# Weights split one chunk ahead, a third block of the MLP in seven products, and the scheduler's order at both ends of the MLP

## The chip, the cores and the metric

The kernel runs on one core of one Trainium2 chip. The metric is the device time of one execution in microseconds (us), lower is better. The time before is the median of three runs.

## The reference

A two-layer transformer for one sequence of T = 256 tokens, width D = 2048, all in float32. Layer 0 mixes with stick-breaking attention, layer 1 with native sparse attention; each is followed by an MLP with 4 x 2048 = 8192 hidden channels.

```python
def sqrelu_mlp(h, w1, w2):
    return jnp.square(jax.nn.relu(h @ w1)) @ w2

def reference(x, ...):
    h = x
    for layer in range(DEPTH):                    # DEPTH = 2
        if layer % N_MIXERS == 0:
            h = h + stick_breaking_attention(rms_norm(h, ...), sb_w_qkv, sb_w_out)
        else:
            h = h + native_sparse_attention(rms_norm(h, ...), nsa_w_in, ..., nsa_w_out)
        h = h + sqrelu_mlp(rms_norm(h, mlp_norm_g[layer]), mlp_w1[layer], mlp_w2[layer])
    return h
```

The change touches the two MLPs and the few microseconds before and behind them.

## The kernel before

**Chunks.** All weights stream through the core once, in chunks of 512 KB: 256 rows of the contraction (KC = 2 tiles of 128) by 512 columns (NB). SP issues the load of a chunk into a `raw` buffer (five) or, in the MLPs, by turns into a `more` buffer (three). A float32 chunk is then split in two: ACT writes the rounded part `hi`, DVE the rest `lo` = raw - hi (function `split`, L143 and L145). There are four buffers of each. PE multiplies hi by both parts of the activations and lo by the high part, so a chunk is three products. With activations x = `xs` (normed input, high and low part) or `yhi`, `ylo` (squared hidden channels) there are three kinds of chunk:

- a chunk of w1 (`chunk_T`, L207): 24 matmuls of 256 columns, 16 with hi and 8 with lo, into two PSUM banks of the pool `acc`;
- a plain chunk of w2 (`chunk_N`, L174): 12 matmuls of 512 columns, 8 with hi and 4 with lo, into two banks of `acc`;
- a seven-product chunk of w2 (`chunk_S`, L270): the chunk's 2 x 2 blocks (two contraction tiles, two halves of the columns) against the 2 x 2 blocks of the activations (two contraction tiles, two halves of the tokens), multiplied as Strassen and Winograd do with 7 products instead of 8: 21 matmuls of 256 columns. DVE first forms four sums of the weight blocks (`ts`, L246 to L250). Three blocks are split as they are (`shi` on ACT, `slo` on DVE, one buffer each), the four sums as a chunk is (`hi<-ts`, `lo<-ts`). The sums of the activations, `ss`, come from the function `high`. The products lie in half banks of four banks of the pool `att`; `add_S` combines them and adds them to h.

**The MLP.** The hidden channels are taken in four groups (fg) of 2048. A group has four blocks of w1 (T, 8 chunks each) and four blocks of w2 (by 512 output columns, nb, 8 chunks each). After a w1 block come the activations: `relu` and `square` on ACT, `high` (ACT and four sums on DVE), `low` and `low7` (ACT and DVE). In groups 0 to 2 blocks 2 and 3 of w2 are seven-product ones, block 0 is plain, and block 1 is half and half: four seven-product chunks in `att`, four plain ones in `acc`. In the last group only block 2 has seven products. When a block is done, `sum2` (plain) or `sum7` (seven-product) adds it to h.

**The order** of PE, DVE, ACT and SP within an MLP is the order in which the code is written (`tc.manual_schedule`); a program's scheduler sets it elsewhere, and POOL's everywhere. `plan` writes it: a list of plain chunks, and a table `after` that says what follows the chunk at each position, a seven-product chunk or a step (a Python call) of the activations and sums. Each group has two lists. The first has w1's blocks 1 to 3 of the group, with the group before's block 3 of w2 among them. The second has block 0 of w2, the next group's block 0 of w1 and the plain chunks of block 1, with the seven-product chunks of blocks 1 and 2 among them. A chunk is loaded, split and multiplied in one go, so that on ACT and DVE its split stands behind every step that was written before its matmuls.

**Work beside it.** While one stage ends, the next one's input is made: `next_x` squares h for the norm (ACT, `junk`, L350), PE transposes h in pieces (`make_x`, L329), ACT and DVE write `xs` from them (L334, L336). `pump` lets one such piece in at the end of each half of a chunk. This happens at the start of an MLP, with the last 512 columns of the stage before, and at the end of the first MLP for the layer that follows.

Of the kernel before, what the change touches and what calls it, by code (L numbers as in the profile page):

```python
# [10 lines left out]
AF = mybir.ActivationFunctionType  # L11
OP = mybir.AluOpType
# [25 lines left out]
JUNK = 1  # L38
SLOPES = [2.0 ** (-8.0 * (i + 1) / NH) for i in range(NH)]
# [3 lines left out]
def hybrid_kernel(  # L43
# [125 lines left out]
    def chunk_N(ps, src, k0, n0, first, last, ahi, alo, koff=0, by_token=False, turn=False):  # L169
# [4 lines left out]
        mm = lambda a, b, k, t, s, e: nc.tensor.matmul(ps[t], a[:, k, t * P:(t + 1) * P], b, start=s, stop=e)  # L174
# [62 lines left out]
    def chunk_S(ps, src, k0, n0, first, last, ahi, alo, shi, slo, koff=0):  # L237

# [13 lines left out]
        thi, tlo = split(ts)  # L252
        k = k0 - koff
# [18 lines left out]
        for i, xh, xl, wh, wl in trivial + sums:  # L272

            mm(i, xh, wh, first and i in (0, 1, 6, 4), False)
            mm(i, xl, wh, False, False)
# [5 lines left out]
    def banks_S(pool, tag):  # L281

        W = NB // 2
        bs = [bank(pool, tag) for _ in range(4)]
        half = lambda j, i: bs[j][:, i * W:(i + 1) * W]
        return bs, [half(0, 0), half(1, 0), half(1, 1), half(2, 0), half(2, 1), half(3, 1), half(3, 0)]

    def add_S(nb, bs, ps, pool, scale):
# [5 lines left out]
        nc.scalar.activation(u[:, 0, :], ps[0], AF.Copy)  # L294
        nc.vector.tensor_tensor(v[:, 0, :], ps[5], u[:, 0, :], op=OP.add)
        nc.vector.tensor_tensor(u[:, 1, :], ps[4], v[:, 0, :], op=OP.add)
        nc.vector.tensor_tensor(v[:, 1, :], ps[6], v[:, 0, :], op=OP.add)
        f0, f1 = scale[:, 0:1], scale[:, 1:2]
        add = lambda o, x, f: nc.vector.scalar_tensor_tensor(o, x, f, o, op0=OP.mult, op1=OP.add)
        add(hb[0], bs[1], f0)  # L300
        add(hb[1], bs[2], f1)
        add(hb[0], u.rearrange("p a n -> p (a n)"), f0)
        add(hb[1].rearrange("p (a n) -> p a n", a=2), v[:, 1, :].unsqueeze(1).to_broadcast([P, 2, W]), f1)
# [114 lines left out]
    def mlp(l, layer, junk, done, last=None):  # L418
# [11 lines left out]
        def chunk1(fg, fb, i):  # L430
            if i == 0:
                banks["T", fb] = [bank(acc, "acc") for _ in range(KB // 2)]
            chunk_T(banks["T", fb], w1, i * KC, fg * D + fb * NB, i == 0, i == NK - 1)
# [33 lines left out]
        def chunk2(fg, nb, i, first, end, turn, by_token=False):  # L467
            if first:
                banks["N", nb] = [bank(acc, "acc") for _ in range(NT)]
            chunk_N(banks["N", nb], w2, fg * KD + i * KC, nb * NB, first, end, yhi, ylo, koff=fg * KD,  # L470
                    by_token=by_token, turn=turn)

        def chunk7(fg, nb, i, first, end):
            if first:
                banks["S", nb] = banks_S(att, "att")
            chunk_S(banks["S", nb][1], w2, fg * KD + i * KC, nb * NB, first, end, yhi, ylo, ss[:, 0], ss[:, 1],
                    koff=fg * KD)

# [3 lines left out]
        def sum7(nb):  # L482
            add_S(nb, *banks["S", nb], junk, factor)

        def plan():
# [17 lines left out]
            def Ss(fg, nb, at, after, ks=range(NK)):  # L503
                for i, j in zip(ks, at):
                    after.setdefault(j, []).append(("S", fg, nb, i, i == ks[0], i == ks[-1]))
# [11 lines left out]
            half = NK // 2  # L517
            for fg in range(NG):
# [683 lines left out]
```

## Time and profile before

| | |
|---|---|
| median of 3 runs | 2160.49 us (2158.95 to 2161.11) |
| the profiled execution's own time | 2155.24 us |
| its span, first to last instruction | 2153.5 us |
| granted TensorE clock, mean | 0.998 |
| busy: PE, DVE, ACT | 2134.2, 1654.2, 1232.2 us |
| moved by DMA | 406.38 MB, mean 189 GB/s |
| seven-product chunks | 136 of 512 in the MLPs |

The span is cut by stages: attention until about 391 us, the first MLP from there to about 1080, the sparse attention to about 1465, and the second MLP to the end. In rows of groups and of the timeline, out<-in are the tiles written and read, then partitions x elements; the number in brackets is the engine's idle time just before and what ended it. Matmuls overlap in their rows (0.28 us for one of 256 columns), so what one costs is read from the starts.

### The profile page before, as it was taken

The page shows a single profiled execution, that of the slowest core. Times are in us where ns is not written, and L with a number is a line of the kernel's source. Part 1 is how long each engine was busy: PE and PEld are TensorE (multiplying, and loading weights), DVE is VectorE, ACT ScalarE, POOL GpSimd, SP SyncE. Part 2 cuts the span into 40 slices and gives each one's busy share as a digit, 9 for nine tenths or more (in the row PEclk, how much of TensorE's full clock was granted, in tenths as well). Part 3 has the DMA queues.
Part 4 walks back from the last instruction along what each step waited for, and adds up shares of the span by engine and source line. Part 5 has one row for each costly group of instructions (what it writes and reads, how often), then busy time and mean ns, then how long its engine had stood idle before and what let it go on. Part 6 is the DMA issues. An engine that isn't in the chain of part 4 may idle for free. (4 is left out here: it accounts for less than half of the span.)

```text
span 2153.5 us, 37647 instructions
## 1 busy us (share of the span) xinstructions
PE 2134.2 (99%) x15110; PEld 1979.8 (92%) x15110; DVE 1654.2 (77%) x2269; ACT 1232.2 (57%) x1683; POOL 45.5 (2%) x78
## 2 busy tenths in 40 slices
PE   9999999999999999999999999999999999999999
PEld 9999988899999999999898888888999999999997
DVE  5556556468989989889687888764589889899896
ACT  6555665455565565565455666654555655655653
POOL 0000000000000000000000100000000000000000
PEclk9999999999999999999999999999999999999999
DMA  7655555566766666666477554455657666666663
GB/s 238 211 169 176 160 182 178 184 202 184 213 196 200 201 205 196 197 214 199 144 197 219 168 145 137 147 189 157 203 185 213 196 200 205 203 197 198 208 214 118
DMA packets 260407, 406.38 MB, mean 189 GB/s; under 512 B 13188, under 2 KB 91912, under 8 KB 260232
## 3 DMA queue, kind: packets, MB, share of 16 engines
q1 hardware_dynamic: 258984, 401.95, 60.6%
q8 instruction: 118, 1.93, 0.4%
q0 software_dynamic: 432, 1.57, 0.2%
q10 hardware_dynamic: 816, 0.46, 0.1%
q14 instruction: 57, 0.47, 0.1%
HBM read 401.83 MB, written 2.10 MB: 188 GB/s over the span
## 5 line engine op out<-in xcount | busy, mean ns | idle before, releaser
L145 DVE TENSOR_TENSOR lo<-raw,hi 128x1024 fp32r<-128x1024 f32 x486 | 590.1, 1221 | 210.8 <-ACT hi L143 201.5
L143 ACT ACTIVATE hi<-raw 128x1024 fp32r<-128x1024 f32 x486 | 509.8, 1054 | 291.5 <-PE acc L174 122.4
L207 PE MATMUL acc<-xs,hi 128*128 128x256 f32 x5360 | 667.3, 277 | 8.3 <-ACT hi L143 7.7
L207 PEld LDWEIGHTS acc<-xs,hi 128*128 128x128 f32 x5360 | 635.9, 188 | 10.2 <-ACT hi L143 8.8
L207 PE MATMUL acc<-xs,lo 128*128 128x256 f32 x2680 | 361.4, 278 | 0.0
L207 PEld LDWEIGHTS acc<-xs,lo 128*128 128x128 f32 x2680 | 331.4, 189 | 0.0
L174 PE MATMUL acc<-hi,yhi 128*128 128x512 f32 x732 | 287.1, 392 | 2.9 <-ACT hi L143 2.9
L174 PE MATMUL acc<-hi,ylo 128*128 128x512 f32 x732 | 285.6, 390 | 0.0
L143 ACT ACTIVATE hi<-ts 128x1024 fp32r<-128x1024 f32 x136 | 144.3, 1061 | 186.8 <-DVE ts L250 185.3
L174 PE MATMUL acc<-lo,yhi 128*128 128x512 f32 x732 | 198.5, 392 | 1.1 <-DVE lo L145 1.1
L145 DVE TENSOR_TENSOR lo<-more,hi 128x1024 fp32r<-128x1024 f32 x129 | 157.4, 1220 | 45.9 <-ACT hi L143 45.2
L145 DVE TENSOR_TENSOR lo<-ts,hi 128x1024 fp32r<-128x1024 f32 x136 | 166.4, 1223 | 23.9 <-ACT hi L143 22.8
L174 PE MATMUL acc<-hi,xs 128*128 128x512 f32 x704 | 177.8, 392 | 0.0
L174 PEld LDWEIGHTS acc<-hi,yhi 128*128 128x128 f32 x732 | 137.4, 188 | 29.4 <-ACT hi L143 3.3
L174 PEld LDWEIGHTS acc<-lo,yhi 128*128 128x128 f32 x732 | 136.5, 188 | 29.8 <-DVE lo L145 2.0
L174 PEld LDWEIGHTS acc<-hi,ylo 128*128 128x128 f32 x732 | 137.5, 188 | 26.0 <-DVE ylo L316 0.2
L143 ACT ACTIVATE hi<-more 128x1024 fp32r<-128x1024 f32 x129 | 135.7, 1052 | 36.3 <-PE acc L207 21.1
L174 PEld LDWEIGHTS acc<-hi,xs 128*128 128x128 f32 x704 | 130.1, 188 | 26.0
L248 ACT ACTIVATE shi<-raw 128x768 fp32r<-128x768 f32 x73 | 61.8, 846 | 103.3 <-PE att L270 103.3
L270 PE MATMUL att<-hi,ss 128*128 128x256 f32 x816 | 114.6, 276 | 0.0
L248 ACT ACTIVATE shi<-more 128x768 fp32r<-128x768 f32 x63 | 53.2, 844 | 97.0 <-PE att L270 97.0
L270 PEld LDWEIGHTS att<-hi,ss 128*128 128x128 f32 x816 | 102.6, 188 | 0.0
(256 smaller groups left out, 2627.5 us busy)
## 6 DMA issues: line engine op xcount, KB each, us to landing
raw<-in_mlp_w_dram SPq DMA_DIRECT2D x320, 512.0 KB, 4.1
more<-in_mlp_w_dram SPq DMA_DIRECT2D x192, 512.0 KB, 4.1
raw<-in_sb_w_qkv_dram SPq DMA_DIRECT2D x95, 512.0 KB, 4.1
raw<-in_nsa_w_in_dram SPq DMA_DIRECT2D x50, 512.0 KB, 3.9
raw<-in_sb_w_out_dram SPq DMA_DIRECT2D x32, 512.0 KB, 4.2
raw<-in_nsa_w_in_dram SPq DMA_DIRECT2D x64, 256.0 KB, 3.8
raw<-in_nsa_w_out_dram SPq DMA_DIRECT2D x32, 512.0 KB, 3.6
w1t<-in_nsa_cmp_w_dram SPq DMA_DIRECT2D x8, 512.0 KB, 4.2
```

What stands on the lines that cost most here:

```text
L143: nc.scalar.activation(hi, raw, AF.Copy)
L145: nc.vector.tensor_tensor(lo, raw, hi.bitcast(F32), op=OP.subtract)
L174: mm = lambda a, b, k, t, s, e: nc.tensor.matmul(ps[t], a[:, k, t * P:(t + 1) * P], b, start=s, stop=e)
L207: nc.tensor.matmul(o, w, x[:, k0 + kk, :], start=s, stop=e, skip_group_check=True)
L248: nc.scalar.activation(hi, flat[:, :3 * W], AF.Copy)
L270: nc.tensor.matmul(ps[i], a, w, start=s, stop=e, skip_group_check=True)
```

## The change

1. `JOINT`: block 1 of w2 in groups 0 to 2 has six seven-product chunks and two plain ones, and the plain ones add to the same banks of `att` (the two whole banks that hold products for one half of the tokens each). One product moves to another half bank for it, and `add_S` makes one addition more in a joint block. The plain block's bank pair for block 1, and its `sum2`, are gone in those groups.
2. `prepare` and `multiply`: the load and split of a chunk are written one chunk ahead of its matmuls, before the steps that follow the chunk in between. Of a seven-product chunk the sums, `shi` and `slo` are written with the chunk before, and its `hi<-ts`, `lo<-ts` behind the split of the next plain chunk.
3. The first eight chunks of w1 in an MLP, and the first MLP's end from position 17 of its last list on (`FREE`), stand in the scheduler's order.
4. `plan`: the next group's block 0 of w1 (eight chunks) now stands behind block 1's plain chunks, and two chunks of the next group's block 1 of w1 follow it; the tables `after` are new. Block 2's last seven-product chunk goes to the next list. In the second MLP's last list `sum2(1)` and `sum7(2)` go one and two positions later.

What the order of the instructions shows. ACT where the first MLP starts; `hi` are the splits of weights, `xs` the next input's pieces, which need PE's transposes, `junk` the squares for the norm. Before:

```order
L143 ACTIVATE hi<-raw 128x1024 x2
L350 ACTIVATE junk,ssq<-h 128x512 x2
L143 ACTIVATE hi<-raw 128x1024
L334 ACTIVATE xs<-att,gT 128x256 x2
L143 ACTIVATE hi<-more 128x1024
L334 ACTIVATE xs<-att,gT 128x256 x2
L143 ACTIVATE hi<-raw 128x1024 x2
```

And now:

```order
L145 ACTIVATE hi<-raw 128x1024 x3
L145 ACTIVATE hi<-more 128x1024
L145 ACTIVATE hi<-raw 128x1024
L366 ACTIVATE junk,ssq<-h 128x512 x2
L145 ACTIVATE hi<-raw 128x1024
L145 ACTIVATE hi<-more 128x1024
L350 ACTIVATE xs<-att,gT 128x256 x2
L145 ACTIVATE hi<-raw 128x1024
L350 ACTIVATE xs<-att,gT 128x256 x2
```

Four more splits stand ahead of the first `xs`; PE's own order is the same there as it was.

ACT at the end of the first MLP, where `uv` is the first step of the sum of block 2. Before:

```order
L294 ACTIVATE uv<-att 128x256
L143 ACTIVATE hi<-raw 128x1024
L350 ACTIVATE junk,ssq<-h 128x512 x2
L143 ACTIVATE hi<-raw 128x1024
L334 ACTIVATE xs<-att,gT 128x256 x4
L143 ACTIVATE hi<-more 128x1024
```

And now:

```order
L145 ACTIVATE hi<-raw 128x1024 x2
L145 ACTIVATE hi<-more 128x1024
L304 ACTIVATE uv<-att 128x256
L145 ACTIVATE hi<-raw 128x1024
L366 ACTIVATE junk,ssq<-h 128x512
L145 ACTIVATE hi<-more 128x1024
L350 ACTIVATE xs<-att,gT 128x256 x4
```

Three splits stand ahead of `uv` now, where one did (the row above the first shown), and the squares are apart.

DVE from block 1's last seven-product chunk (`lo<-ts`) on to block 2, in the first group; `uv` and the `h` rows are the block's sum, `h<-acc` that of block 0. Before:

```order
L145 TENSOR_TENSOR lo<-ts,hi 128x1024
L145 TENSOR_TENSOR lo<-raw,hi 128x1024
L145 TENSOR_TENSOR lo<-more,hi 128x1024
L145 TENSOR_TENSOR lo<-raw,hi 128x1024
L295 TENSOR_TENSOR uv<-att,uv 128x256
L296 TENSOR_TENSOR uv<-att,uv 128x256
L297 TENSOR_TENSOR uv<-att,uv 128x256
L299 SCALAR_TENSOR_TENSOR h<-att,factor,h 128x512 x2
L299 SCALAR_TENSOR_TENSOR h<-uv,factor,h 128x512 x2
L145 TENSOR_TENSOR lo<-more,hi 128x1024
L387 SCALAR_TENSOR_TENSOR h<-acc,factor,h 128x512 x2
L145 TENSOR_TENSOR lo<-raw,hi 128x1024
```

And now:

```order
L147 TENSOR_TENSOR lo<-ts,hi 128x1024
L147 TENSOR_TENSOR lo<-raw,hi 128x1024
L147 TENSOR_TENSOR lo<-more,hi 128x1024
L403 SCALAR_TENSOR_TENSOR h<-acc,factor,h 128x512 x2
L147 TENSOR_TENSOR lo<-raw,hi 128x1024
L306 TENSOR_TENSOR uv<-att,uv 128x256
L307 TENSOR_TENSOR uv<-att,uv 128x256
L309 TENSOR_TENSOR uv<-att,uv 128x256
L310 TENSOR_TENSOR uv<-att,uv 128x256
L302 SCALAR_TENSOR_TENSOR h<-att,factor,h 128x512 x2
L302 SCALAR_TENSOR_TENSOR h<-uv,factor,h 128x512 x2
L249 TENSOR_TENSOR ts<-raw 128x512
```

The sum of block 0 now stands ahead of that of block 1, only three plain chunks' `lo` lie between the two seven-product chunks up to block 2's first sums, and block 1's sum has one row more (L310).

The diff, cut to its core:

```diff
+JOINT = (1,)
+FREE = "the scheduler's order from here"
...
-    def chunk_S(ps, src, k0, n0, first, last, ahi, alo, shi, slo, koff=0):
+    def prepare_S(src, k0, n0):
...
         nc.vector.tensor_tensor(lo, flat[:, :3 * W], hi.bitcast(F32), op=OP.subtract)
-        thi, tlo = split(ts)
+        return hi, lo, ts
+
+    def chunk_S(ps, parts, k, first, last, ahi, alo, shi, slo, starts):
+        W = NB // 2
+        hi, lo, thi, tlo = parts
...
-    def banks_S(pool, tag):
+    def banks_S(pool, tag, joint):
         W = NB // 2
         bs = [bank(pool, tag) for _ in range(4)]
-        return bs, [half(0, 0), half(1, 0), half(1, 1), half(2, 0), half(2, 1), half(3, 1), half(3, 0)]
+        at = [(0, 0), (1, 0), (1, 1), (2, 0), (0, 1) if joint else (2, 1), (3, 1), (3, 0)]
+        return bs, [bs[j][:, i * W:(i + 1) * W] for j, i in at], (0, 1, 6, 3 if joint else 4)
...
+        if joint:
+            nc.vector.tensor_tensor(v[:, 0, :], ps[6], v0, op=OP.add)
+            nc.vector.tensor_tensor(v[:, 1, :], ps[6], u[:, 1, :], op=OP.add)
...
+        def prepare(c, follower):
+            if c[0] == "T":
+                fg, fb, i = c[1:]
+                return load_split(w1, i * KC, KC, fg * D + fb * NB, NB, o=(FAR, FAR))
+            fg, nb, i = c[1:4]
+            where = w2, fg * KD + i * KC
+            if c[0] == "S":
+                return prepare_S(*where, nb * NB)
+            gap = PAD - FAR if follower in ("T", "S") else 0
+            return load_split(*where, KC, nb * NB, NB, o=(FAR, FAR), gap=gap)
+
+        def multiply(c, parts):
...
+            joint = nb in JOINT and fg < NG - 1
...
+            if joint:
+                ps = banks["S", nb][0][1:3]
...
-            half = NK // 2
+            mix = NK - 2
...
-                    plain = sum([Ts(fg, fb) for fb in range(1, NF)], [])
-                    put(after, 2, do(sum7, 2))
-                    put(after, 3, do(sum2, 1))
-                    Ss(fg - 1, 3, (3, 5, 7, 10, 13, 15, 18, 21), after)
-                    stages(after, 8, 0, True)
+                    plain = (Ts(fg, 1) + Ts(fg, 2) + Ts(fg, 3))[2:]
+                    Ss(fg - 1, 2, (0,), after, (NK - 1,))
+                    put(after, 3, do(sum7, 2))
+                    Ss(fg - 1, 3, (5, 7, 9, 11, 13, 15, 17, 19), after)
+                    stages(after, 9, 0, True)
                     stages(after, 13, 1)
-                    stages(after, 18, 2)
+                    stages(after, 17, 2)
...
-                    plain = Ns(fg, 0) + Ts(fg + 1, 0) + Ns(fg, 1, range(half, NK))
-                    Ss(fg, 1, (4, 5, 6, 7), after, range(half))
-                    put(after, 10, do(sum7, 1))
+                    plain = Ns(fg, 0) + Ns(fg, 1, range(mix, NK)) + Ts(fg + 1, 0) + Ts(fg + 1, 1)[:2]
+                    Ss(fg, 1, (4, 5, 6, 7, 8, 9), after, range(mix))
                     put(after, 11, do(sum2, 0))
-                    Ss(fg, 2, (12, 13, 14, 15, 16, 17, 18, 19), after)
-                    put(after, 18, do(relu, 0))
+                    put(after, 12, do(sum7, 1, True))
+                    Ss(fg, 2, (13, 14, 15, 16, 17, 18, 19), after, range(NK - 1))
+                    put(after, 19, do(relu, 0))
...
+                if c == ("T", 0, 1, 0):
+                    order.enter_context(tc.manual_schedule(engines={
+                        mybir.EngineType.PE, mybir.EngineType.DVE, mybir.EngineType.Activation, mybir.EngineType.SP
+                    }))
+                if c == FREE:
+                    order.close()
...
+                    following = None
+                    if c1 and c1[0] != "S":
+                        following = prepare(c1, follower)
+                    if c[0] == "S":
+                        parts = *parts[:2], *split(parts[2])
+                    if c1 and c1[0] == "S":
+                        following = prepare(c1, follower)
+                    multiply(c, parts)
+                    parts = following
```

More of the change, by code (lines that the diff above doesn't have):

```diff
@@ L272, in chunk_S @@
         for i, xh, xl, wh, wl in trivial + sums:
-            mm(i, xh, wh, first and i in (0, 1, 6, 4), False)
+            mm(i, xh, wh, first and i in starts, False)
             mm(i, xl, wh, False, False)
@@ L428, in factors @@
             nc.vector.tensor_tensor(factor, r, r, op=OP.mult)
[L430 to L433, printed above, removed]
+        def prepare(c, follower):
[9 more added lines that the diff above has]
+        def multiply(c, parts):
+            if c[0] == "T":
+                fg, fb, i = c[1:]
+                if i == 0:
+                    banks["T", fb] = [bank(acc, "acc") for _ in range(KB // 2)]
+                chunk_T(banks["T", fb], parts, i * KC, 0, i == 0, i == NK - 1)
+                return
+            fg, nb, i, first, end = c[1:6]
+            joint = nb in JOINT and fg < NG - 1
+            if c[0] == "S":
+                if first:
+                    banks["S", nb] = banks_S(att, "att", joint)
+                _, ps, starts = banks["S", nb]
+                chunk_S(ps, parts, i * KC, first, end, yhi, ylo, ss[:, 0], ss[:, 1], starts)
+                return
+            tail = last is not None and (fg, nb) == (NG - 1, 3)
+            if joint:
+                ps = banks["S", nb][0][1:3]
+            else:
+                if first:
+                    banks["N", nb] = [bank(acc, "acc") for _ in range(NT)]
+                ps = banks["N", nb]
+            chunk_N(ps, parts, i * KC, 0, first and not joint, i == NK - 2 if tail else end, yhi, ylo,
+                    by_token=tail and end, joint=joint)
         def relu(fb):
@@ L465, in low7, with sum7 @@
             nc.vector.tensor_tensor(o[:, 1], part["q", fb], o[:, 0].bitcast(F32), op=OP.subtract)
[L467 to L477, printed above, removed]
         def sum2(nb):
             add_h(nb, banks["N", nb], factor)
-        def sum7(nb):
-            add_S(nb, *banks["S", nb], junk, factor)
+        def sum7(nb, joint=False):
+            bs, ps, _ = banks["S", nb]
+            add_S(nb, bs, ps, joint, junk, factor)
         def plan():
@@ L552, in plan @@
                 yield from merge(plain, after)
         spawn(factors(), 1)
-        with tc.manual_schedule(engines={mybir.EngineType.PE, mybir.EngineType.DVE, mybir.EngineType.Activation,
-                                         mybir.EngineType.SP}):
-            steps = list(plan())
-            for n, c in enumerate(steps):
-                if callable(c):
-                    c()
-                    continue
-                follower = next((d[0] for d in steps[n + 1:] if not callable(d)), None)
-                if c[0] == "T":
-                    chunk1(*c[1:])
-                elif c[0] == "S":
-                    chunk7(*c[1:])
-                elif last is not None and c[1:3] == (NG - 1, 3):
-                    fg, nb, i, first, end = c[1:]
-                    chunk2(fg, nb, i, first, i == NK - 2, False, end)
-                else:
-                    chunk2(*c[1:], turn=follower in ("T", "S"))
+        steps = list(plan())
```

47 lines of the change are left out of this document (32 added, 15 removed).

## The prediction

> **What bounds the kernel now.** I read the page first (busy shares, slices), then the waits of PE over the whole run, then PE, clock and DVE in the stretches that those waits point to, and last the instructions one by one. Two engine lines of the page, PE and DVE:
>
> ```profile
> span 2153.5 us, 37647 instructions
> PE 2134.2 (99%) x15110; PEld 1979.8 (92%) x15110; DVE 1654.2 (77%) x2269; ACT 1232.2 (57%) x1683; POOL 45.5 (2%) x78
> ```
>
> PE is the bound nearly everywhere. So the time can fall in two ways only: fewer columns through PE, or the places where PE stands still. All waits of PE from the list of waits (total, times, longest):
>
> ```profile
> PE acc L207 <- ACT hi L143: 7.7, 5, 1.9
> PE acc L174 <- ACT hi L143: 2.9, 2, 1.9
> PE acc L174 <- DVE lo L145: 1.1, 2, 0.6
> PE acc L207 <- ACT xs L334: 0.6, 1, 0.6
> ```
>
> These four are 12.3 us and nearly all that PE ever waits for weights. The stretches that hold them (columns: length, then busy PE, PEld, DVE, ACT, POOL, then the granted clock PEclk, DMA share, GB/s):
>
> ```profile
> 391.00:412.00 21.00, 17.25 (x128) 16.26 (x127) 11.50 (x17) 10.08 (x16) 0.70 (x1) 0.92 0.38 105
> 480.00:570.00 90.00, 90.00 (x650) 84.16 (x649) 77.02 (x98) 50.38 (x57) 0.00 (x0) 1.00 0.64 194
> 1061.00:1092.00 31.00, 26.98 (x173) 23.36 (x172) 22.07 (x34) 20.03 (x39) 4.72 (x13) 1.00 0.45 128
> 1465.00:1487.00 22.00, 18.06 (x124) 17.36 (x123) 11.20 (x16) 9.94 (x16) 0.69 (x1) 0.84 0.36 100
> 2131.00:2150.00 19.00, 18.10 (x91) 14.96 (x89) 10.66 (x15) 5.24 (x6) 0.72 (x1) 1.00 0.09 34
> ```
>
> 391 and 1465 are the starts of the two MLPs, 1061 and 2131 their ends. 480 to 570 lies inside an MLP: PE never stops there, while DVE is busy 77.0 of 90 us. So inside the MLP DVE is the engine next in line, and no wait stands there to be removed. At the starts the clock is also lowered: 0.92 over 21 us is 1.7 us lost, 0.84 over 22 us is 3.5 us.
>
> How one such wait comes about, PE first and then ACT, in the first MLP:
>
> ```profile
> 397.51 0.60 PE L329 MATMUL att<-ident,h 128*128 128x128 f32 x4
> 399.98 2.10 PE L207 MATMUL acc<-xs,hi 128*128 128x256 f32 x16 [1.87 <-ACT hi L143]
> 402.82 0.60 PE L329 MATMUL att<-ident,h 128*128 128x128 f32 x4
> 405.30 2.91 PE L207 MATMUL acc<-xs,hi 128*128 128x256 f32 x16 [1.87 <-ACT hi L143]
> 408.00 1.90 PE L207 MATMUL acc<-xs,lo 128*128 128x256 f32 x8
> ...
> 393.56 1.05 ACT L143 ACTIVATE hi<-raw 128x1024 fp32r<-128x1024 f32 x1
> 398.14 0.84 ACT L334 ACTIVATE xs<-att,gT 128x256 fp32r<-128x256 f32 x2 [3.54 <-PE att L329]
> 398.87 1.05 ACT L143 ACTIVATE hi<-more 128x1024 fp32r<-128x1024 f32 x1
> ```
>
> ACT is idle for 3.54 us in front of `xs`, which needs PE's transposes, and the next chunk's `hi` stands behind it. PE finishes the transposes and then waits for both. Four transposes that nothing holds up take 0.36 us to the next matmul, as the end of the first MLP shows:
>
> ```profile
> 1065.17 0.60 PE L329 MATMUL att<-ident,h 128*128 128x128 f32 x4
> 1065.53 1.18 PE L174 MATMUL acc<-lo,yhi 128*128 128x512 f32 x4
> ```
>
> From 397.51 to 399.98 are 2.47 us, so one such wait costs 2.1 us and not the 1.87 printed. After the second one 16 matmuls take 2.91 us and eight take 1.90 instead of 2.10 and about 1.07: that is the half clock of the window row.
>
> **The change, part by part.** (1) Twelve plain chunks of w2 (two in each of three groups of two MLPs) become seven-product ones. The price of each on PE, by starts:
>
> ```profile
> 541.16 0.28 PE L270 MATMUL att<-shi,yhi 128*128 128x256 f32 x1
> ...
> 543.54 1.98 PE L207 MATMUL acc<-xs,hi 128*128 128x256 f32 x16
> 545.35 1.07 PE L207 MATMUL acc<-xs,lo 128*128 128x256 f32 x8
> 546.26 0.28 PE L270 MATMUL att<-shi,yhi 128*128 128x256 f32 x1
> ```
>
> A seven-product chunk takes 543.54 - 541.16 = 2.38 us, a chunk of w1 with 24 matmuls of 256 columns 2.72; a plain chunk of w2 streams the same columns as 12 of 512. 12 x 0.34 = **4.1 us less**, all of it on PE, the bound. Its DVE price is below.
>
> (2) Splits one chunk ahead, and the scheduler's order in the first eight chunks. The rows of ACT in the part on the change show four more `hi` ahead of the first `xs`. Then PE has its next weights when the transposes end. All five waits of L207 for `hi` lie at the two starts; I expect them gone: 7.7 us, and 0.24 more for each of the four long ones, 8.7 us, and with them the two half-clock stretches, 1.7 + 3.5 = 5.2 us. **13.9 us less.** The cover is the four `hi` buffers: the split for a chunk waits until PE has let go of the fourth before it. PE takes 2.72 us a chunk and ACT 1.05, so it is early even with `xs` (0.84) and the squares between. The loads go one chunk earlier on SP's queue with the splits and wait for the same buffers; DMA's share of 0.64 in 480 to 570 leaves them room.
>
> (3) The released order at the end of the first MLP: waits 0.6 (`lo`, behind the seven-product block's sum on DVE), two on `hi` (2.9 together) and 0.6 on `xs` at the next layer's start, each some 0.2 longer from start to start: 4.7 us. The new ACT rows have two `hi` ahead of each `xs` there. I leave 1 us for a wait of which only the place changes: **3.7 less.** In the second MLP the block's sum moves two chunks later, behind splits that are already done: the 0.6 (0.7 with its restart) goes. **0.7 less.** The outputs' DMAs, on POOL's queue, go with it two chunks (5.4 us) later; the last chunk's own DMAs still end the run, so that costs nothing.
>
> (4) What it adds to DVE. Its rows for one pair of plain and seven-product chunk, and the sums of blocks:
>
> ```profile
> 536.31 0.68 DVE L246 TENSOR_TENSOR ts<-more 128x512 f32<-128x512 f32 x1
> 537.02 0.42 DVE L249 TENSOR_TENSOR ts<-ts,more 128x256 f32<-128x256 f32 x1
> 537.48 0.42 DVE L250 TENSOR_TENSOR ts<-more,ts 128x256 f32<-128x256 f32 x1
> 538.26 0.96 DVE L251 TENSOR_TENSOR slo<-more,shi 128x768 fp32r<-128x768 f32 x1 [0.35 <-PE att L270]
> 539.13 1.22 DVE L145 TENSOR_TENSOR lo<-ts,hi 128x1024 fp32r<-128x1024 f32 x1
> 540.27 1.22 DVE L145 TENSOR_TENSOR lo<-raw,hi 128x1024 fp32r<-128x1024 f32 x1
> 541.41 0.68 DVE L246 TENSOR_TENSOR ts<-more 128x512 f32<-128x512 f32 x1
> ...
> 517.56 0.42 DVE L295 TENSOR_TENSOR uv<-att,uv 128x256 f32<-128x256 f32 x1
> 521.39 1.22 DVE L145 TENSOR_TENSOR lo<-more,hi 128x1024 fp32r<-128x1024 f32 x1
> 522.53 1.41 DVE L387 SCALAR_TENSOR_TENSOR h<-acc,factor,h 128x512 f32<-128x512 f32 x2
> 523.85 1.22 DVE L145 TENSOR_TENSOR lo<-raw,hi 128x1024 fp32r<-128x1024 f32 x1
> ```
>
> By starts: `lo` 1.14, seven-product chunk 3.6 without the wait, its block's sum 3.83 (4.17 with the joint block's one more addition of 0.34), a plain block's sum 1.32. A pair is 4.75 of DVE against 5.10 of PE. The second part of a group has 20 plain and 13 seven-product chunks afterwards (12 before): PE 20 x 2.72 + 13 x 2.38 = 85.3 us; DVE 22.8 + 46.8, sums 3.8 + 4.2 + 1.3, and one block of activations, at most 4 (four sums of L249's size, 0.42 each, and two of a `lo`'s): 82.9. It stays under PE, by 2.4 us. The ten moved chunks of w1 cost the same where they are now. The third block of w1 follows its bank's relu by one position and not three; ACT does that relu more than a chunk ahead, so I cost it at nothing; if the cover went, PE would wait there for two ACT instructions of half a `hi`'s size, 1 us. The exchange of `lo` and `lo<-ts` in DVE's row brings the latter 1.14 later, into 0.3 us after PE begins the chunk; PE needs it 1.93 after (541.16 to 543.09, behind 17 matmuls of 0.113).
>
> The tight place is where block 2 begins. Count from PE's start of block 1's last seven-product chunk: PE has that one (2.38) and four plain ones, so block 2 starts at 13.26 and wants its `lo<-ts` at 15.19. DVE: from 0.25 two `lo` (2.5), the plain sum (3.85); the next `lo` waits for the fourth buffer before it, until PE ends its first plain chunk (5.1, and 0.3 to be told), and ends its slot at 6.5; joint sum 10.7; preparation 13.2; another `lo` 14.3; `lo<-ts` done 15.5. PE waits 0.3, 0.4 with its restart, six times: **2.4 more.** From below it is 0 (DVE half a microsecond earlier); from above 1.5 a place, if one more `lo` of 1.14 gets in front: 9. I take 2.4, worked from rows of the same operations.
>
> Sum: -4.1 - 13.9 - 3.7 - 0.7 + 2.4 = **-20.0 us**. The profiled execution (2155.24, of which the span is 2153.5) would be 2135.2. It lies 5.2 below the median of the runs, 2160.49; taken from that, **2140.5**.
>
> **The rivals.**
>
> A. One wait stays at each MLP start, because a split stands between the two `xs` and its buffer is not free when ACT reaches it. For it: ACT's list still has one `hi` between them. Against: PE lets that buffer go a chunk before. It would give back two waits of 2.1 and half of the clock term, 6.8: 2147.3.
>
> B. The half clock is not the waits' doing, and stays when they go. Against: the clock is 1.00 in all quiet windows. For: the first wait of 1.87 at 399.98 has full speed behind it, and so has the one at the end of the MLP (1061 to 1092: 1.00). It gives back 5.2: 2145.7. The Trainium skill (TensorE: Matmul & The Clock Gate, What's actually happening) states this rule: the clock drops after an idle window of about 3.4 us, free-running. By that rule no gap of 1.87 would do it alone; the trace has half clock right behind the gap that ends at 405.30, so it disagrees on the length, and the free phase may be why not behind all.
>
> C. Slower: DVE becomes the bound in the second parts. In the trace it idles there beside its work: 0.35 a pair for PE's release of the one `slo` buffer, and more behind a block's sum, some 9 in 83 us if the 13 us without work of 480 to 570 are put down to such waits in good part. Were these to stay with the work at 82.9, a part would take 92 instead of 85.3, 6.6 more, six times 39, less the 2.4 counted: 2177. It decides from 4 us a part (24 in all). Against: the waits are for PE, and shrink as DVE falls behind.
>
> D. The change does not do what it says: the waits move to where the order now has `xs` or the block's sum, and DVE's lag eats the 4.1. About 2158, no change.
>
> **How the numbers follow.** Forecast 0.66, A 0.15, B 0.10, D 0.05, C 0.04. About 0.2% (4.3 us) is what a measurement of this kernel tells from no change. Forecast, A and B are all faster by more: 0.91; D is the same: 0.05; C slower: 0.04. The range goes from 2136 (no new wait at all, 2.4, and the 1 us, with 1 for the runs' spread) to 2149 (A, or the new waits at their upper end of 9, with as much): C and D are outside.
>
> **What would show it.** Right: PE's waits for `hi`, `lo` and `xs` in the four stretches under 2 us together, PEclk 1.00 at both MLP starts, 252 more seven-product matmuls and 144 fewer plain ones, DVE's busy time up by some 30 us (12 x 2.46), and six waits of PE for `lo` of 0.3 to 0.5 us where block 2 starts. Wrong: a new row of PE waiting for DVE of more than 9 us, or 1.87 waits still behind the transposes.

## The result, and the profile after

The changed kernel takes **2132.2 us** (median of 4 runs, 2131.97 to 2132.36), beside 2159.7 for the kernel before (4 runs, 2155.8 to 2161.1): ratio 0.9875 [0.9858, 0.9892]. Forecast were 2140.5, within 2136 to 2149. The direction held, and so did the mechanism of the two largest terms; the time came out 8.3 us below the forecast, which is 3.8 below the range. The profiled execution took 2132.3, of which the span is 2130.6; the one before had 2155.24 and 2153.5.

The engine lines of the page of the changed kernel:

```profile
span 2130.6 us, 37899 instructions
PE 2122.5 (100%) x15218; PEld 1976.5 (93%) x15218; DVE 1673.6 (79%) x2311; ACT 1238.5 (58%) x1695; POOL 45.9 (2%) x78
```

PE was busy for 2134.2 of 2153.5 us and is now for 2122.5 of 2130.6: 19.3 us stood still or were out of any row before, 8.1 are now. DVE has 19.4 us more work, and still a fifth of the span free. All waits of PE in its list (total, times, longest):

```profile
PE att L644 <- POOL ident masks.py:199: 1.6, 1, 1.6
PE att L947 <- DVE a L938: 1.1, 1, 1.1
PE att L918 <- DVE hs L913: 0.6, 1, 0.6
PE acc L663 <- ACT hi L656: 0.5, 1, 0.5
PE att L965 <- DVE kc L960: 0.4, 1, 0.4
PE att L953 <- DVE ga L942: 0.2, 1, 0.2
```

The lines L211, L176 and L277 (the chunks of the MLPs; L207, L174 and L270 before) are not in it at all. What is left belongs to the two attentions and the program's start. The stretches that answer to the five of before (start of MLP 1, inside it, its end, start of MLP 2, the end; columns as there):

```profile
391.00:412.00 21.00, 21.00 (x183) 20.58 (x182) 11.83 (x17) 11.18 (x16) 0.70 (x1) 1.00 0.61 178
480.00:570.00 90.00, 90.00 (x675) 85.20 (x674) 81.97 (x107) 49.92 (x58) 0.00 (x0) 1.00 0.61 196
1054.00:1085.00 31.00, 31.00 (x222) 28.65 (x221) 24.17 (x40) 18.90 (x34) 5.09 (x13) 1.00 0.54 159
1447.00:1469.00 22.00, 22.00 (x166) 20.92 (x165) 12.46 (x17) 11.53 (x16) 0.70 (x1) 1.00 0.62 180
2108.00:2127.00 19.00, 18.72 (x99) 15.93 (x97) 9.57 (x14) 3.61 (x5) 1.46 (x2) 1.00 0.16 61
```

PE fills both starts (17.25 of 21 and 18.06 of 22 before), with a granted clock of 1.00 in place of 0.92 and 0.84. The rows at the first start, PE and then ACT:

```profile
397.20 0.60 PE L345 MATMUL att<-ident,h 128*128 128x128 f32 x4
397.56 2.07 PE L211 MATMUL acc<-xs,hi 128*128 128x256 f32 x16
...
387.95 1.06 ACT L145 ACTIVATE hi<-more 128x1024 fp32r<-128x1024 f32 x1 [1.71 <-PE acc L176]
...
396.49 1.06 ACT L145 ACTIVATE hi<-more 128x1024 fp32r<-128x1024 f32 x1 [1.66 <-PE acc L211]
397.84 0.84 ACT L350 ACTIVATE xs<-att,gT 128x256 fp32r<-128x256 f32 x2 [0.29 <-PE att L345]
399.67 1.06 ACT L145 ACTIVATE hi<-raw 128x1024 fp32r<-128x1024 f32 x1 [0.99 <-PE acc L211]
```

From the transposes to the next matmul are 0.36 us where 2.47 were. The `hi` of 396.49 is for a later chunk: it waited for PE to let go of a buffer, so the other three of the four held the splits of the next three chunks. These are the three rows of `hi` before it, and the first of them, that of 387.95, is for the matmul at 397.56; it was done 8 us before PE transposes. ACT still stands in front of `xs`, for 0.29 us and not for 3.54, and nothing of PE's stands behind it.

Where the 22.9 us of span went, by the starts of the first and last seven-product matmul of each MLP in the two traces:

| stretch | before | after | difference | forecast |
|---|---|---|---|---|
| start of the run to MLP 1's first | 499.55 | 493.34 | -6.2 | -6.0 (half of the starts' waits, 4.3, and 1.7 of clock) |
| MLP 1, first to last | 557.38 | 555.10 | -2.3 | -2.0, and +1.2 of new waits |
| MLP 1's last to MLP 2's first | 517.77 | 506.50 | -11.3 | -11.5 (3.7, 4.3 and 3.5) |
| MLP 2, first to last | 557.44 | 555.10 | -2.3 | -2.0, and +1.2 of new waits |
| MLP 2's last to the end | 21.40 | 20.56 | -0.8 | -0.7 |

Of the signs that the forecast named, the waits for weights are gone from the four stretches, the clock is 1.00 at both starts, and PE has 252 seven-product matmuls more and 144 plain ones fewer. The six waits for `lo` and the 30 us on DVE did not come.

### The profile page after: what moved, and what is told of

It reads as the page before. It is cut to its first block, busy times and chain, and to the rows that moved or that the text cites. A ratio compares the mean times of both kernels' runs of the same rounds, so it can differ in the third digit from the quotient of the medians.

```text
span 2130.6 us, 37899 instructions
## 1 busy us (share of the span) xinstructions
PE 2122.5 (100%) x15218; PEld 1976.5 (93%) x15218; DVE 1673.6 (79%) x2311; ACT 1238.5 (58%) x1695; POOL 45.9 (2%) x78
## 4 chain that ended last, share of the span: by engine, by line
PE 98%; DVE 1%; issue 0%; ACT 0%; DMA 0%; POOL 0%; DVEq 0%; SPq 0%; ACTq 0%; POOLq 0%
PE acc L211 43%; PE acc L176 30%; PE att L277 17%; PE att L176 3%; PE att L1073 1%; PE att L345 1%; PE att L784 0%; PE att L736 0%; DVE lo L147 0%; PE att L1011 0%; PE att L1013 0%; PE att L1067 0%; PE att L1012 0%; PE att L1066 0%; PE att L1065 0%
## 5 line engine op out<-in xcount | busy, mean ns | idle before, releaser
L147 DVE TENSOR_TENSOR lo<-raw,hi 128x1024 fp32r<-128x1024 f32 x468 | 569.9, 1222 | 213.5 <-ACT hi L145 200.2
L145 ACT ACTIVATE hi<-raw 128x1024 fp32r<-128x1024 f32 x468 | 493.4, 1055 | 330.2 <-PE acc L176 141.6
L211 PE MATMUL acc<-xs,hi 128*128 128x256 f32 x5360 | 665.0, 277 | 0.0
L211 PEld LDWEIGHTS acc<-xs,hi 128*128 128x128 f32 x5360 | 633.9, 188 | 0.4
L211 PE MATMUL acc<-xs,lo 128*128 128x256 f32 x2680 | 359.1, 276 | 0.0
L211 PEld LDWEIGHTS acc<-xs,lo 128*128 128x128 f32 x2680 | 329.1, 188 | 0.0
L176 PE MATMUL acc<-hi,yhi 128*128 128x512 f32 x636 | 249.6, 393 | 0.0
L176 PE MATMUL acc<-hi,ylo 128*128 128x512 f32 x636 | 248.1, 390 | 0.0
L251 ACT ACTIVATE shi<-raw 128x768 fp32r<-128x768 f32 x91 | 77.0, 846 | 212.6 <-PE att L277 206.1
L176 PE MATMUL acc<-hi,xs 128*128 128x512 f32 x704 | 177.8, 392 | 0.0
L176 PE MATMUL acc<-lo,yhi 128*128 128x512 f32 x636 | 172.5, 392 | 0.0
L176 PEld LDWEIGHTS acc<-hi,xs 128*128 128x128 f32 x704 | 130.1, 188 | 25.9
L176 PEld LDWEIGHTS acc<-lo,yhi 128*128 128x128 f32 x636 | 118.6, 188 | 24.2
L176 PEld LDWEIGHTS acc<-hi,ylo 128*128 128x128 f32 x636 | 119.5, 188 | 23.2 <-DVE ylo L332 0.2
L176 PEld LDWEIGHTS acc<-hi,yhi 128*128 128x128 f32 x636 | 119.4, 188 | 23.0 <-ACT yhi L331 0.2
L277 PE MATMUL att<-hi,ss 128*128 128x256 f32 x888 | 124.7, 276 | 0.0
L254 DVE TENSOR_TENSOR slo<-raw,shi 128x768 fp32r<-128x768 f32 x91 | 87.0, 956 | 45.2 <-PE att L277 44.2
L277 PEld LDWEIGHTS att<-hi,ss 128*128 128x128 f32 x888 | 111.6, 188 | 0.0
```

What stands on the lines that cost most here:

```text
L145: nc.scalar.activation(hi, raw, AF.Copy)
L147: nc.vector.tensor_tensor(lo, raw, hi.bitcast(F32), op=OP.subtract)
L211: nc.tensor.matmul(o, w, x[:, k0 + kk, :], start=s, stop=e, skip_group_check=True)
L251: nc.scalar.activation(hi, flat[:, :3 * W], AF.Copy)
L254: nc.vector.tensor_tensor(lo, flat[:, :3 * W], hi.bitcast(F32), op=OP.subtract)
L277: nc.tensor.matmul(ps[i], a, w, start=s, stop=e, skip_group_check=True)
```

## The experiments

**The kernel before, traced twice more.** No edit. The profiled execution of before lay 5.2 us below the median, and the forecast took it that the changed kernel's would too.

> The kernel before once more, for its spread: its four runs lie at 2155.8 to 2161.1 us, those of the changed kernel within 0.4 us of each other. Theory W (the spread is half clock behind PE's waits, which falls differently in each execution): an execution near 2160 has a granted clock under 1.00 in more than the two MLP starts, or for longer there, and the extra loss is about 5 us (10 us at half clock); one near 2155 looks like the trace before. Theory R (the spread has another source, such as memory): the clock rows are as in the trace before (0.92 and 0.84), and the 5 us lie elsewhere, as longer waits or slower transfers.

> The same again, for a second execution. W: time and time at half clock go together, 1 us of time for 2 us at half clock. R: they don't.

Measured: 2157.95 and 2159.21. Half clock came in two stretches of 3.41 us in each of these traces, in three in the first one, and not behind the same waits. So both executions had less half clock than the first one and were still 2.7 and 4.0 us longer: neither theory fits whole. What differs shows in the stretch 1500 to 1560 (MLP 2's first group, only chunks of w1). It is given here with two rows of one chunk in it, from the first trace of before and then from the second:

```profile
1500.00:1560.00 60.00, 60.00 (x532) 60.00 (x531) 38.69 (x42) 32.48 (x34) 0.00 (x0) 1.00 0.67 199
...
1522.99 1.98 PE L207 MATMUL acc<-xs,hi 128*128 128x256 f32 x16
1524.81 1.07 PE L207 MATMUL acc<-xs,lo 128*128 128x256 f32 x8
```

```profile
1500.00:1560.00 60.00, 60.00 (x511) 60.00 (x511) 37.81 (x41) 31.44 (x33) 0.00 (x0) 1.00 0.62 191
...
1524.21 2.05 PE L207 MATMUL acc<-xs,hi 128*128 128x256 f32 x16
1526.09 1.10 PE L207 MATMUL acc<-xs,lo 128*128 128x256 f32 x8
```

Both have PE busy for all 60 us at a granted clock of 1.00, and yet the second gets 4% fewer matmuls through. Sixteen take 2.05 us and not 1.98; from start to start it is 117.8 ns a matmul instead of 113.3. In the two further traces this slower pace lasts from about 1485 to 1565, 3 us lost, and again from about 1092 to 1122, 1 us lost. So one execution of the kernel before differs from the next by how many stretches of half clock (1.7 us each) and how much of the slower pace it met. Its 38 runs in this study go from 2149.98 to 2164.51. The 2149.98 has a mean clock of 1.000 and no half clock: 2155.24 less three times 1.7 is 2150.1.

**Splits ahead and the scheduler's ends alone**, with the plan and the banks of before (136 seven-product chunks).

```diff
-JOINT = (1,)
+JOINT = ()
...
-            mix = NK - 2
+            half = NK // 2
...
```

> Splits one chunk ahead and the scheduler's order at both ends of the MLP, but the plan, the banks and the 136 seven-product chunks of the kernel before. W: the waits at the starts and ends go (13.9 + 4.7 + 0.7 us of the profiled execution) and the spread with them, so the median falls by 23 to 24.5 us, to about 2136, with runs within 1 us. R: the spread stays, and the median falls by 19, to about 2141.

Measured: 2136.0 (2135.5 to 2136.2), ratio 0.9909 [0.9886, 0.9932], span 2134.4, clock 1.000. PE's list has only lines of the attentions and the start:

```profile
span 2134.4 us, 37643 instructions
PE att L645 <- POOL ident masks.py:199: 1.6, 1, 1.6
PE att L948 <- DVE a L939: 1.0, 1, 1.0
...
PE att L966 <- DVE kc L961: 0.4, 1, 0.4
```

The median and the closeness of the runs are those that the first theory gave. The span is 19.1 shorter than before; forecast were 18.3 for this part (13.9, 3.7 and 0.7). From here to the full change the span loses 3.8 and the median 3.8, against the 4.1 of the first term. The two were not run side by side; the full change's two medians, the second from another chip than this kernel's, differ by 0.01.

**The new plan and the joint banks alone**: each chunk split in one go with its multiplication, everything in written order.

```diff
-                    following = None
-                    if c1 and c1[0] != "S":
-                        following = prepare(c1, follower)
+                    parts = prepare(c, chunks[0][1])
...
-                if c == ("T", 0, 1, 0):
+                if n == 0:
```

> The new plan with the third block in 6/8 seven products and joint banks, but each chunk split in one go and the whole MLP in the written order, as before. Both theories: the waits of 2 us at the MLP starts stay; 4.1 us less from 12 chunks and at most 0.7 at the end: 2155 to 2156 against 2160, a ratio of 0.998. W: the runs keep a spread of some 5 us. A theory that the joint plan costs DVE time (2.4 us of waits where block 2 starts): 2158, with PE waiting for lo there.

Measured: 2166.0 (2158.7 to 2173.2, 10 runs), ratio 1.0046 [1.0029, 1.0062]: 12 cheaper chunks, and slower than before (2156.6 beside it). The expectations of 2155 to 2158 all missed. Its waits, and the same stretch at MLP 1's start:

```profile
PE acc L211 <- ACT hi L145: 7.7, 5, 1.9
PE acc L176 <- ACT hi L145: 4.5, 3, 1.9
PE acc L176 <- DVE lo L147: 2.2, 1, 2.2
...
391.00:412.00 21.00, 17.25 (x129) 16.29 (x128) 11.60 (x17) 10.15 (x16) 0.70 (x1) 0.92 0.36 107
```

The starts are as before; at MLP 1's end PE waits longer (the four rows of before are 12.3 us together, these three 14.4), which takes back half of the 4.1. Half clock takes more: the granted clock is 0.9963 in the mean of its ten runs and 0.9982 in the 13 of before beside them, some 4 us. With the cheaper chunks this makes 2 of the 9.4 us between the medians. The rest I put down to the slower pace, but only the profiled execution, the fastest of the ten, shows it: it runs from 1820 to 1901, after two starts that come 0.15 and 0.23 us behind the one before and not 0.11, while PE waits for `hi` of a chunk's sums. That is too short for the list.

**The full change without the scheduler, and without the splitting ahead.** The first has the whole MLP in written order; the second splits each chunk in one go and leaves the two ends to the scheduler (each one half of the diff above).

> The changed kernel with the whole MLP in the written order, so splits ahead but no scheduler's order at the ends. If splitting ahead is what removes the waits at the starts: no wait of 1.9 us there, and most of the 13.9 us stay gone; at the first MLP's end the sums in the written order (position 17) may leave a wait of PE for lo of up to 2.4 us as in joint_only: 2133 to 2137, runs close together. If the scheduler's order is what does it: the four waits of 1.9 us are back and the runs spread, 2145 to 2155.

> The changed kernel with each chunk split in one go again, but the scheduler's order for the first eight chunks and at the first MLP's end. If the scheduler's order alone removes the waits at the ends: they are gone, and the time depends on the short waits inside the MLP for hi<-ts that joint_only has, each followed by up to 80 us at the slower pace: 2135 to 2150, with a spread. If splitting ahead is needed at the ends too: waits of 1.9 us are back.

Measured: 2132.73 (2132.3 to 2133.6) without the scheduler, ratio 0.988 [0.9859, 0.9901]; 2137.2 without splitting ahead (2134.2 to 2141.9), ratio 0.9895 [0.9868, 0.9923]. Neither has a wait of the MLPs in its list. So either half of the change removes the waits at the ends by itself. With the splits ahead the scheduler's order adds nothing that these runs can tell. What splitting ahead does beyond that is inside the MLP, in the second kernel's trace at 700, where the sums' `hi` is late:

```profile
699.69 0.39 PE L277 MATMUL att<-shi,ss 128*128 128x256 f32 x2
700.05 0.97 PE L277 MATMUL att<-hi,ss 128*128 128x256 f32 x6
...
701.92 2.05 PE L211 MATMUL acc<-xs,hi 128*128 128x256 f32 x16
```

Two matmuls should take 0.23 us and took 0.36, the six behind them 0.97 and not 0.84; then the slower pace (2.05) holds for 118 us, about 5 us lost with the pause, and once more from 1767.

**Waits put in.** To the changed kernel, 16 times (eight in each MLP, among the first group's chunks of w1): a transpose, one copy on ACT (then five), a transpose of that. The results are not used.

```diff
+            nc.tensor.transpose(ps[:, :P], h[:, 0, :P], ident)
+            nc.scalar.activation(g[:, :P], ps[:, :P], AF.Copy)
...
+            nc.tensor.transpose(ps[:, P:2 * P], g[:, :P], ident)
```

> The changed kernel with 16 waits put in (eight in each MLP, behind every third chunk of w1 blocks 1 to 3 of the first group): PE transposes a piece of h, ACT copies it (128 x 128), PE transposes the copy and goes on. The output is not touched. PE should stand still some 0.5 us each time: 2132 plus 16 x 0.7 is 2143 if that were all. Theory P (two paces): in joint_only a wait of 0.15 us at 1820 is followed by 80 us in which a matmul of 256 columns takes 117.8 ns instead of 113.3, at full granted clock; so behind some of the 16 the pace changes and stays until something else disturbs PE, up to 4% of 170 us, 7 us more. Without P: 113.3 ns everywhere. No half clock in either.

> The same with five copies in a row on ACT, so waits of some 1.5 to 2 us, like those of the kernel before. 2132 plus 16 x 2 is 2164. Theory W: some of the 16 are followed by 3.4 us at half clock (1.7 us each), as two or three of four are in the kernel before: 2166 to 2190. Rival (the clock needs an idle stretch of about 3.4 us, as the Trainium skill has it in TensorE: Matmul & The Clock Gate, What's actually happening): none, 2164.

Measured, one execution each: 2148.95 with 16 waits of 0.4 us, at a clock of 1.000: no half clock, but the slower pace in parts of both first groups. 2173.07 with 16 waits of 1.8 us (28.3 together): half clock behind two of the sixteen. The first of the two:

```profile
493.70 0.27 PE L524 MATMUL att<-ident,h 128*128 128x128 f32 x1
495.77 0.33 PE L528 MATMUL att<-ident,ping 128*128 128x128 f32 x1 [1.80 <-ACT ping L527]
495.86 3.30 PE L211 MATMUL acc<-xs,hi 128*128 128x256 f32 x16
```

So waits are what half clock follows, but not each of them. The trace's clock records tell more. In each trace the changes of the clock lie on one grid of 3.41 us steps, and the grid begins at another point of the program in each execution (its lines lie 0.16, 2.90 and 0.65 us after multiples of 3.41 in the three traces of before). Five traces have half clock while PE is at work: the three of before, the one with the joint banks alone, and this one with waits of 1.8 us. They have 38 pauses of 1.73 us or more. 21 of them are cut by a line of the grid, and none of these has half clock behind it. 17 fall whole into one step, and behind 12 of these the next step is at half clock (behind 10 of 11 in the kernels without put-in waits, behind 2 of 6 here). So it matters how a pause lies on the grid, and the same wait of the kernel before has half clock behind it in one execution and not in the next.

**DVE delayed where block 2 starts.** The forecast had PE waiting there for `lo<-ts`, six times, and the trace after shows no wait. DVE and then PE at the first of the six places:

```profile
521.53 1.40 DVE L403 SCALAR_TENSOR_TENSOR h<-acc,factor,h 128x512 f32<-128x512 f32 x2
522.85 1.21 DVE L147 TENSOR_TENSOR lo<-raw,hi 128x1024 fp32r<-128x1024 f32 x1
523.98 0.42 DVE L306 TENSOR_TENSOR uv<-att,uv 128x256 f32<-128x256 f32 x1
...
528.20 0.69 DVE L249 TENSOR_TENSOR ts<-raw 128x512 f32<-128x512 f32 x1
...
531.73 1.22 DVE L147 TENSOR_TENSOR lo<-ts,hi 128x1024 fp32r<-128x1024 f32 x1
...
532.31 0.28 PE L277 MATMUL att<-shi,yhi 128*128 128x256 f32 x1
...
534.24 0.50 PE L277 MATMUL att<-lo,ss 128*128 128x256 f32 x3
```

`lo<-ts` is done at 532.95, PE wants it at 534.24: 1.3 us to spare. To test that, two and four more additions of 128x512 on DVE, behind the block's sum, with results that nobody reads; beside them the changed kernel once more.

```diff
+                nc.vector.tensor_tensor(g, h[:, 0, :NB], h[:, 1, :NB], op=OP.add)
...
-                    put(after, 12, do(sum7, 1, True))
+                    put(after, 12, do(sum7, 1, True), do(drag))
```

> The changed kernel once more, beside the three below on the same chip. If its times really lie close together (0.4 us in the first four runs), 2132.2 within 0.5 again, with a profiled execution like the others and a clock of 1.000 throughout. If that closeness was chance, runs 2 to 5 us longer turn up.

> The changed kernel with two more DVE additions of 128x512 (some 0.66 us each by starts, 1.3 together; their results are not used) written behind block 1's sum, six places. Theory from the trace after (the last lo<-ts is done 1.3 us before PE wants it where block 2 starts): no wait or one of 0.1 to 0.2 us, 2132 to 2134. The prediction's count (PE waits there already): 6 x 1.3 = 8 more, 2140.

> The same with four additions, 2.6 us a place. Theory (1.3 us to spare): PE waits 1.3 to 1.5 us for lo in six places, 8 to 9 more, 2140 to 2141, and up to 2 more each where such a wait starts half clock or the slower pace. The prediction's count: 6 x 2.6 = 16 more, 2148. If DVE as a whole were the bound in these parts, both kernels with additions would cost their full 8 and 16.

Measured: 2132.19 for the changed kernel (2132.0 to 2132.9); 2141.84 with two additions and 2146.12 with four, one execution each. By the time alone the forecast's count seems to have been right (2140 for two). The rows say otherwise. With two, PE's chunk at 532.3 takes 2.59 us from start to start, 0.21 more than the 2.38 without, so six places make 1.3 us. With four:

```profile
532.63 0.39 PE L277 MATMUL att<-shi,ss 128*128 128x256 f32 x2
533.67 0.96 PE L277 MATMUL att<-hi,ss 128*128 128x256 f32 x6 [0.65 <-ACT hi L145]
...
535.64 0.61 PE L277 MATMUL att<-lo,ss 128*128 128x256 f32 x3 [0.44 <-DVE lo L147]
...
536.20 1.98 PE L211 MATMUL acc<-xs,hi 128*128 128x256 f32 x16
```

The chunk began at 532.18 and takes 4.02, 1.64 more, which are the 2.64 of DVE less 1.3 to spare, plus two restarts and DVE's lag handed on; times six, 9.8 us. The rest of both times is the slower pace: 8.7 us in two stretches of 116 us (702 to 818, 1935 to 2051) with two additions, 4.4 in one (1939 to 2055) with four. The end of the first stretch, with two:

```profile
815.37 2.05 PE L211 MATMUL acc<-xs,hi 128*128 128x256 f32 x16
817.25 1.10 PE L211 MATMUL acc<-xs,lo 128*128 128x256 f32 x8
818.20 0.39 PE L176 MATMUL acc<-hi,yhi 128*128 128x512 f32 x1
818.42 0.39 PE L176 MATMUL acc<-hi,ylo 128*128 128x512 f32 x1
```

From the first plain chunk of w2 on, the first with matmuls of 512 columns, the pace is the faster one again (0.23 us for 512 columns). All eight long stretches inside the MLPs end in such a chunk: these three, the two without splitting ahead, the one with joint banks alone, and one in each further trace of before. So a pause that starts the slower pace costs 4% of the way to the next plain chunk of w2.

**Is it the wait, the work, or chance?** The kernel with two additions once more, and one with the same additions at the end of each first part of a group, where PE does not wait for DVE:

```diff
-                    put(after, 12, do(sum7, 1, True), do(drag))
+                    put(after, 12, do(sum7, 1, True))
...
+                    put(after, 21, do(drag))
```

> The kernel with two added DVE additions at six places once more. In its first run PE lost 0.2 us at each of six places (1.3) and ran 4% slower for some 120 us behind two of them (8.5 together). Theory (a short wait starts the slower pace by chance): the times fall on steps of about 4.3 us above 2133.5 (2133.5, 2137.8, 2142.1, 2146.4), and the profiled run shows other places than the first. Rival (place or data decide it): every run within 1 us of 2141.8, with the slower pace at 700 to 820 and 1930 to 2060 again.

> The same two DVE additions, six times, but at the end of each first part of a group, where DVE has time to spare and PE should not wait for it. If PE's waits start the slower pace: none of it, 2132.2 within 0.5, as without the additions. If more work on DVE starts it, or lengthens its queue: above 2134, spread as the other's.

Measured: 2133.12 (2132.9 to 2133.3) with the waits, ratio 0.9885 [0.987, 0.9899], and 2131.93 (2131.7 to 2132.5) where the same work is covered. Neither theory of the first expectation fits whole: the places do not decide it, but the times are not spread over steps either; all four stand on the lowest. PE's rows around 701, in the first execution and in this one:

```profile
701.18 0.28 PE L277 MATMUL att<-slo,ss 128*128 128x256 f32 x1
701.37 0.62 PE L277 MATMUL att<-lo,ss 128*128 128x256 f32 x3
...
701.95 2.05 PE L211 MATMUL acc<-xs,hi 128*128 128x256 f32 x16
```

```profile
701.17 0.28 PE L277 MATMUL att<-slo,ss 128*128 128x256 f32 x1
701.38 0.61 PE L277 MATMUL att<-lo,ss 128*128 128x256 f32 x3
...
701.94 1.98 PE L211 MATMUL acc<-xs,hi 128*128 128x256 f32 x16
```

The same instructions with the same pause (0.2 us from start to start and not 0.11), and behind it 2.05 us in the one, for 116 us, and 1.98 in the other. The one took 2141.84 us and the other 2133.1. They ran on two chips; whether the chip or chance made the difference is open. On a single chip the kernel without splitting ahead, with pauses of that size, went from 2134.2 to 2141.9 at a clock of 1.000 in all four runs, so chance within one chip is likely; only the longest of the four has a trace to show the slower pace.

**One chunk further.** Seven seven-product chunks and one plain one in the joint block, three moved chunks of block 1 of w1 instead of two, block 2's last two seven-product chunks in the next list:

```diff
-            mix = NK - 2
+            mix = NK - 1
...
-                    Ss(fg - 1, 2, (0,), after, (NK - 1,))
+                    Ss(fg - 1, 2, (0, 1), after, (NK - 2, NK - 1))
...
-                    put(after, 12, do(sum7, 1, True))
-                    Ss(fg, 2, (13, 14, 15, 16, 17, 18, 19), after, range(NK - 1))
+                    put(after, 13, do(sum7, 1, True))
+                    Ss(fg, 2, (14, 15, 16, 17, 18, 19), after, range(NK - 2))
```

> The changed kernel with seven seven-product chunks and one plain one in block 1 of groups 0 to 2 (six and two before), three chunks of block 1 of w1 moved instead of two, and block 2's last two seven-product chunks in the next list. Six plain chunks become seven-product ones. Theory of the sum's first term (0.34 us a chunk, all of it on PE, DVE hidden): -2.0 us, to 2130.2. Rival (DVE is now the bound in the second parts, or the denser row of seven-product chunks lets PE wait, and a wait starts the slower pace): same or slower than the changed kernel, 2132 to 2138.

Measured: **2129.02** (2128.97 to 2129.09), ratio to the kernel before 0.9868 [0.9854, 0.9883], beside 2132.19 for the changed kernel on the same chip: 3.2 less, and the fastest version here. From first to last seven-product matmul each MLP takes 553.96 us and not 555.10, 2.3 less for both (2.0 expected). Most of the rest lies between MLP 1's last seven-product matmul and MLP 2's first, which this edit does not touch: 505.50 us here and 506.19 in the changed kernel's trace from the same chip. Eight other traces with neither the long waits nor put-in ones have 506.05 to 506.50 there. So this is more than their spread, and why is not shown.

## Why the prediction was right or wrong

**The offset to the median: the step that failed most, 5.2 of the 8.3 us.** "It lies 5.2 below the median of the runs, 2160.49; taken from that, 2140.5." I took the distance between one execution and the median for a constant of the measurement. It belonged to the kernel: its waits started half clock and the slower pace, and lost more to them in most executions than in the profiled one. It was not even the same everywhere: in the later runs, on four chips, the median of before lies 1.3 to 3.5 above 2155.24. The changed kernel has hardly such waits, its eight runs lie within 0.9 us, and its profiled execution is its median. The forecast for the execution itself was 2135.2 and came out at 2132.3, which leaves 2.9 us for the steps below. The change thus removed those losses too, and I counted only the share that the one trace happened to show.

**The new waits at block 2's start: +2.4, measured 0.** The step was that "the next `lo` waits for the fourth buffer before it, until PE ends its first plain chunk". It did not wait. In the row of 522.85 it stands right behind the plain sum. Three of the four buffers then held parts that PE was still to read for its next three plain chunks (from 523.25, 525.97 and 528.69 on), so this `lo` can only lie where block 1's last `lo<-ts` was, which PE had finished by 521.43, one chunk sooner than the first of the three. I had assumed that buffers go round in the order of writing. The count had this `lo` done 6.5 us after PE's start of block 1's last seven-product chunk, and it was done after 4.9 (519.04 to 523.98). The difference is the whole miss of 1.6 at the end: 15.5 counted for `lo<-ts`, 13.9 measured. The additions on DVE confirm the 1.3 us to spare: two of them (1.3) cost 0.2 a place, four (2.6) cost 1.6.

**1 us for a wait that only moves: not needed.** With this and small differences the ends and starts gave 19.1 and not 18.3. (The four waits at MLP 1's end, each with its 0.2, are 4.9 and not 4.7.)

**The seven-product chunks: right, 4.1 against 3.8** from the one kernel to the other, 4.6 if only the stretches between the first and last of them are taken. DVE's work grew by 19.4 us and not by some 30: I left out that six sums of plain blocks (1.32 each) fall away, 7.9.

**Splits ahead: right, but the cause was split wrongly.** I gave MLP 1's end to the released order. Splitting ahead removes that wait too, and the scheduler's order alone removes those at the starts. The same holds at MLP 2's end, which I gave to the later sums: it takes 20.56 us in the kernel with the splits ahead and the sums at their old places, 20.54 with the later sums and no splits ahead, 21.40 before. The half clock went with the waits, as the sum had it.

**The rivals.** A (a wait stays): no. B (half clock stays): no; the clock is 1.000 in every run of the kernels without these waits, and 16 put-in waits of 1.8 us brought half clock back. The two waits that spoke for B, at 399.98 and at MLP 1's end, are among those that a line of the grid cuts. C (DVE bound): no; 16 us more work for DVE cost what its delay at six places handed to PE, with the slower pace behind one of them, and covered work cost nothing. D (no change): the nearest thing is the plan without the splits, slower by 0.5%.

Still open: what the slower pace is, why one pause starts it and the next doesn't, and why five of the 17 pauses that lie whole in one step of the grid had no half clock behind them.

## What to carry to other kernels

Where an engine is the bound, a pause of it may cost more than its length: look at the start-to-start time of the same instruction in several stretches and in several executions, also where the granted clock says 1.00. Before a sum worked out on one profiled execution is carried over to a median, ask what makes that kernel's executions differ, and whether the change takes it away. A split or load written one step ahead makes a kernel's time not only shorter but steadier, here from 14 us between the lowest and highest of 38 runs to one between those of eight.

## What the runs showed of the hardware

- PE has two paces at a granted clock of 1.00: 113.3 and 117.8 ns from start to start of a 256-column matmul. The slower one begins behind pauses as short as 0.1 to 0.4 us, but not behind every pause. In the traces without put-in waits it lasted 79 to 118 us inside the MLPs, 3 to 5 us lost a time, and ended each time in the first plain chunk of w2 (512 columns) that came. With waits put in, stretches of 3 to 25 us were seen; most ended at a later put-in wait or at such a chunk. All but one of the sixteen traces show it for some 27 us just after the second layer begins, about 1080 to 1127.
- Half clock comes in stretches of 3.41 us (1.7 us lost), behind 2 of 16 pauses of 1.8 us, behind two or three of the waits of that size in each trace of before, and behind none of 16 pauses of 0.4. Of 38 pauses of 1.73 to 2.23 us the 21 that a line of the 3.41 us grid cuts had none behind them, of the 17 that lie whole in one step 12 had. The Trainium skill (TensorE: Matmul & The Clock Gate, What's actually happening) gives about 3.4 us for the idle window; the length of the stretch agrees with that, the pauses that led to it were little over half as long.
